# A hybrid attention and recurrence block: the attention output's norm as a step of its own

## The chip, the cores and the metric

The kernel runs on one core of one Trainium2 chip. The metric is the device time of one execution in microseconds (us); less is better. Five engines work side by side on a core, each through its own queue of instructions, in order: TensorE (PE in the profile; the loads of its stationary operand are listed as PEld), VectorE (DVE), ScalarE (ACT), GpSimd (POOL) and SyncE (SP), which here only issues transfers. They wait for each other through semaphores.

## The reference, cut to what matters

One decoder layer for 512 tokens of width 2048, in float32. The input is normalised and projected once; the columns of the projection go to two head groups, eight heads of dilated attention and eight heads of a gated linear recurrence, and the two outputs are concatenated and projected back.

```python
attn = dilated_attention(aq, ak, av).reshape(B, S, ATTN_WIDTH)   # 512 x 1024
attn = rms_norm(attn, attn_out_norm_w)                           # over all 1024 columns of a token

ho = hgrn2(gq, gf, gi, lb)
hg = rms_norm(ho, hg_norm_w) * silu(gg)                          # per head of 128 columns
mix = concatenate([attn, hg], axis=-1) @ w_out                   # 512 x 2048 times 2048 x 2048
x = x + gate1 * mix
# then a second norm and a squared-ReLU MLP of width 8192, gated and added
```

The change concerns the second line, and when it is done beside the lines under it. What is computed stays the same.

## The kernel before

Tokens stand in four tiles of 128 (`NT`), channels in blocks of 128. Float32 products are made as three matmuls of split operands: each weight block is loaded as `wraw`, rounded by ACT into `whi` (L39), and DVE forms the remainder `wlo` (L40); activations are split into `hi` and `lo` in the same way (`split_to`, L239 and L240). Weight tiles are in rings of four buffers: one load brings the rows of two k steps, and a cast can start as soon as PE has finished with the buffer four k steps back.

A projection (`project`) runs 16 k steps. One k step is twelve matmuls of 128x512 (L198 to L200, four token tiles by three products); here it is called a group. After each group `tick()` advances a list of generators, `tasks`, by one `yield`; the head of the list runs until it ends, then the next begins. So the order of PE's instructions is that of the code, and `tasks` is how the work of the heads is dealt out between the groups. PE's queue is recorded as written (`manual_schedule`); the order on ACT, DVE, POOL and SP is set by a planner that goes by its own costs. A second list, `bgw`, runs the adaLN matrix-vector products in the background: transfers `araw` (L123) and DVE instructions L127 and L129.

Near the place of the change the projections are, in order: the gate of the first recurrent half (`hg_gate(0)`), the gate of the second (`hg_gate(1)`), then the output projection in four quarters (`project_out(q)`). While `hg_gate(1)` runs, the list holds the rest of the second attention half, then `hg_out(0)`, then `attention_out`; `hg_out(1)` is appended behind them.

- `hg_out(half)` lets three ticks pass, multiplies the four heads by the gate on DVE (L718, one instruction for each head and token tile) and hands each head to `to_mix`.
- `attention_out` squares and sums the eight tiles `aq` on ACT (L530), adds the partial sums (L531) and makes the reciprocal root on DVE and POOL (L211, L212), multiplies the eight tiles on DVE (L535), then hands eight heads to `to_mix`, one for each tick.
- `to_mix` transposes a head's four blocks on PE into one bank of PSUM (L545, tile `ptm`, a ring of four banks) and writes it to SBUF as a `mix` block on ACT (L547). `mix` blocks are split in the order 8 to 11 (first recurrent half), 0 to 7 (attention), 12 to 15 (second recurrent half) and are consumed in that order by the 16 groups of `project_out(0)`, which asks for two ticks for each of its first ten groups.

The output tiles of the squares (`jk`, L529) are in the same ring of two buffers, tag `ev`, as the tiles `sg` in which `hg_gate` makes its sigmoids (L706 to L709). At the end of `hg_gate(1)` ACT copies the four banks to `gg` (L703), then makes the sigmoids (L707), and DVE finishes them (L708, L709).

Of the kernel before, what the change touches and what calls it, by code (L numbers as in the profile page):

```python
# [44 lines left out]
def hybrid_block(ctx, tc, x, c, positions, norm1_w, w_ada, b_ada, w_in, q_norm_w, k_norm_w,  # L45
# [164 lines left out]
    def rstd_of(dst, ss, n, inv_n):  # L210
        dve.tensor_scalar(dst, ss, inv_n, EPS, op0=ALU.mult, op1=ALU.add)  # L211
        pool.tensor_tensor(dst, dst, mhalf[:, 0:n], op=ALU.pow)  # L212
# [15 lines left out]
    def slot(name, dt=F32):  # L228
        return io.tile([P, 512], dt, name=name, tag="io")
# [124 lines left out]
    tasks = []  # L354
# [13 lines left out]
    def project(c0, mm, rate=1.85, after=None):  # L368

        banks = [bank("prj", tag="mm") for _ in range(4)]  # L370
        for k0 in range(0, NK, 2):
            for j, (whi, wlo) in enumerate(load_w(win_v, k0, c0, 512, None)):
                k = k0 + j
                mm(banks, hhi[k], hlo[k], whi, wlo, k == 0, k == NK - 1)
                tick()
                owed[0] += rate
                while owed[0] >= 1.0:
                    bg_step()
                    owed[0] -= 1.0
                if after:  # L380
                    after(k)
        return banks
# [55 lines left out]
    def qk(c0, name, i):  # L438
        ts = evac(project(c0, tok_mm), name)
        rs = sm.tile([P, NT, 4], F32, name=f"rs{i}", bufs=2)  # L440
        bgw.insert(0, qk_norm(ts, i, rs))
        return ts if i else (ts, rs)
# [78 lines left out]
        values(3, p_sb, lsum)  # L521
        yield

    def attention_out(aos):
        ssa = sm.tile([P, NT, 2], F32, name="ssa", bufs=1)
        ra = sm.tile([P, NT], F32, name="ra", bufs=1)
        for ti in range(NT):
            for u in range(2):
                jk = wk.tile([P, 512], F32, name="jk", tag="ev", bufs=2)  # L529
                act.activation(jk, aos[u][ti], AF.Square, accum_out=ssa[:, ti, u:u + 1])  # L530
        dve.tensor_reduce(ra, ssa, axis=AX.X, op=ALU.add)  # L531
        rstd_of(ra, ra, NT, 1.0 / 1024)
        for u in range(2):
            for ti in range(NT):
                dve.tensor_scalar(aos[u][ti], aos[u][ti], ra[:, ti:ti + 1], None, op0=ALU.mult)  # L535
        yield
        for u in range(2):
            for h in range(4):
                to_mix(u * 4 + h, aos[u], slice(h * DH, (h + 1) * DH), aoc[:, u * 4 + h:u * 4 + h + 1])
                yield  # L540

    def to_mix(k, src, hs, wcol):
        pt = bank("ptm")
        for ti in range(NT):
            pe.transpose(pt[:, ti * P:(ti + 1) * P], src[ti][:, hs], ident)  # L545
        mix[k] = slot("mix")
        act.activation(mix[k], pt, AF.Identity, scale=wcol)  # L547
# [149 lines left out]
    def hg_gate(ht):  # L697
        gb = project(6144 + ht * 512, tok_mm, after=split_early if ht else None)
        gs = []
        for ti in range(NT):  # L700
            g = slot("gg")
            with tc.high_priority():
                act.copy(g, gb[ti])  # L703
            gs.append(g)
        for g in gs:
            sg = wk.tile([P, 512], F32, name="sg", tag="ev", bufs=2)  # L706
            act.activation(sg, g, AF.Tanh, scale=0.5)  # L707
            dve.tensor_scalar(sg, sg, 0.5, 0.5, op0=ALU.mult, op1=ALU.add)  # L708
            dve.tensor_tensor(g, g, sg, op=ALU.mult)  # L709
        return gs  # L710

    def hg_out(ht, gs, os_, rs):
        for _ in range(3):
            yield
        for h in range(4):
            hs = slice(h * DH, (h + 1) * DH)
            for ti in range(NT):
                dve.scalar_tensor_tensor(gs[ti][:, hs], os_[h][:, ti * P:(ti + 1) * P], rs[:, h, ti:ti + 1],  # L718
                                         gs[ti][:, hs], op0=ALU.mult, op1=ALU.mult)
            yield  # L720
            to_mix(8 + ht * 4 + h, gs, hs, hgc)
# [118 lines left out]
    q0 = qk(0, "aq", 0)  # L840
# [6 lines left out]
    q1 = qk(512, "aq", 0)  # L847
    k1 = qk(1024 + 512, "ak", 1)
    v1 = evac(project(2048 + 512, tok_mm), "av")
    tasks.append(attention(q1, k1, v1))  # L850
    gs = hg_gate(0)
    tasks.append(hg_out(0, gs, f0, hrs[0]))
    tasks.append(attention_out((q0[0], q1[0])))
    gs = hg_gate(1)
    tasks.append(hg_out(1, gs, f1, hrs[1]))
# [547 lines left out]
def _program(arrays):  # L1403
    import concourse.bacc as bacc
    nc = bacc.Bacc("TRN2", target_bir_lowering=False, num_devices=1)
    args = [nc.dram_tensor(n, a.shape, mybir.dt.from_np(a.dtype), kind="ExternalInput").ap()
            for n, a in arrays.items()]
    args.append(nc.dram_tensor("out_0_dram", _OUTS[0][0], F32, kind="ExternalOutput").ap())
    with tile.TileContext(nc, schedule_with_timeline_sim=True) as tc:
        hybrid_block(tc, *args)  # L1410
    return nc
# [10 lines left out]
```

## Time and profile before

| what | before |
|---|---|
| time, median of 3 runs | 2303.53 us (2301.55 to 2304.42) |
| the profiled execution's own time | 2298.58 us |
| its span, first to last instruction | 2296.8 us |
| mean granted TensorE clock | 0.993 |
| PE busy | 2227.1 us (97%) |
| DVE busy | 1810.4 us (79%) |
| ACT busy | 1098.4 us (48%) |
| POOL busy | 444.6 us (19%) |

The span is the time between the core's first and last instruction; 1.8 us of the execution's time lie around it. A page shows each engine's busy time, the span in 40 slices with the clock that PE was granted, the transfer queues, and the chain of work that ended last. The answers of the trace that are used below are: stretches of time with the busy time of each engine in them; instructions in order of time, each with its start, its duration and, in square brackets, how long its engine had stood idle before it and what ended that; and the median time of transfers from issue to landing. A line such as L545 is the line of the kernel before; behind the change these lines stand two or three lower.

### The profile page before, as it was taken

To read this page: it belongs to the slowest core of one execution; us is meant where nothing else is said; L and a number is where in the kernel's file an instruction comes from. 1 tells how busy PE (TensorE), PEld (TensorE's weight loads), DVE (VectorE), ACT (ScalarE), POOL (GpSimd) and SP (SyncE) were. 2 spreads that over 40 slices of the span, in tenths; PEclk is the share of its full clock that TensorE was granted. 3 is DMA by queue.
4 is the path that set the end of the run, shared out by engine and by line. 5 is a ranking of instruction groups with operands and counts; after the bars stand their busy time and mean duration, and the time that the engine had idled before them with its cause. 6 is when DMAs were issued, how large, how long until landed. Compare 5 with 4: busy or idle time off the path is not lost.

```text
span 2296.8 us, 33106 instructions
## 1 busy us (share of the span) xinstructions
PE 2227.1 (97%) x11769; PEld 1825.0 (79%) x11769; DVE 1810.4 (79%) x2765; ACT 1098.4 (48%) x1950; POOL 444.6 (19%) x664
## 2 busy tenths in 40 slices
PE   4999999999999979999999999999999999999999
PEld 3787878878778868888887888888888888788887
DVE  6999778678786574678748988988897779967878
ACT  5555434433444453457544656555564333343332
POOL 1000022000220000002232323323333222222221
PEclk9999999999999989999999999999999999999999
DMA  9798455646555256756969799889889987998784
GB/s 327 254 335 316 129 176 166 198 146 219 168 176 157 73 165 198 249 168 214 371 226 383 255 346 351 297 305 384 301 327 388 344 294 261 379 342 293 276 301 165
DMA packets 262583, 598.31 MB, mean 260 GB/s; under 512 B 23221, under 2 KB 43969, under 8 KB 262417
## 3 DMA queue, kind: packets, MB, share of 16 engines
q1 hardware_dynamic: 186800, 332.54, 43.1%
q0 software_dynamic: 70720, 254.21, 30.0%
q10 hardware_dynamic: 4896, 9.44, 1.2%
q8 instruction: 93, 1.52, 0.3%
q14 instruction: 74, 0.60, 0.1%
HBM read 518.49 MB, written 77.61 MB: 260 GB/s over the span
## 4 chain that ended last, share of the span: by engine, by line
PE 63%; issue 15%; DMA 10%; DVE 7%; POOL 2%; ACT 1%; SPq 0%; POOLq 0%; DVEq 0%; ACTq 0%
PE f L1179 8%; PE f L1180 8%; PE f L1178 8%; PE prj L198 8%; PE prj L199 7%; PE prj L200 7%; DMA f_lod<-fs 2%; PE f L208 2%; PE f L207 2%; PE f L206 2%; DVE vlo L1163 2%; DMA araw<-in_w_ada_dram 2%; PE prj L207 2%; PE prj L208 2%; PE prj L206 1%
## 5 line engine op out<-in xcount | busy, mean ns | idle before, releaser
L1162 ACT CAST vhi<-raw 128x1024 fp32r<-128x1024 f32 x392 | 413.5, 1056 | 536.7 <-PE f L1180 415.7
L1163 DVE TENSOR_TENSOR vlo<-raw,vhi 128x1024 fp32r<-128x1024 f32 x392 | 476.9, 1222 | 152.1 <-ACT vhi L1162 151.2
L1179 PE MATMUL f<-vlo,Fh 128*128 128x512 f32 x1376 | 537.5, 391 | 3.4 <-DVE vlo L1163 3.3
L1180 PE MATMUL f<-vhi,Fl 128*128 128x512 f32 x1376 | 535.7, 389 | 0.8 <-DMA Fl<-f_lod 0.8
L1178 PE MATMUL f<-vhi,Fh 128*128 128x512 f32 x1376 | 536.0, 390 | 0.0
L39 ACT CAST whi<-wraw 128x512 fp32r<-128x512 f32 (+1 forms) x368 | 220.2, 601 | 460.3 <-PE prj L200 315.3
L198 PE MATMUL prj<-whi,hi 128*128 128x512 f32 x896 | 366.1, 409 | 3.7 <-ACT gq L562 2.2
L200 PE MATMUL prj<-whi,lo 128*128 128x512 f32 x896 | 352.0, 393 | 0.0
L199 PE MATMUL prj<-wlo,hi 128*128 128x512 f32 x896 | 351.7, 393 | 0.0
L40 DVE TENSOR_TENSOR wlo<-wraw,whi 128x512 fp32r<-128x512 f32 (+1 forms) x368 | 243.5, 666 | 135.0 <-ACT whi L39 132.3
L129 DVE SCALAR_TENSOR_TENSOR acc<-araw,sc,acc 128x512 f32<-128x512 f32 (+1 forms) x392 | 253.6, 675 | 92.9 <-DMA araw<-in_w_ada_dram 91.8
L1179 PEld LDWEIGHTS f<-vlo,Fh 128*128 128x128 f32 x1376 | 258.2, 188 | 63.4 <-DVE vlo L1163 10.4
L1180 PEld LDWEIGHTS f<-vhi,Fl 128*128 128x128 f32 x1376 | 258.3, 188 | 54.4 <-DMA Fl<-f_lod 1.2
L1178 PEld LDWEIGHTS f<-vhi,Fh 128*128 128x128 f32 x1376 | 258.3, 188 | 53.8
L1146 DVE TENSOR_TENSOR raw<-raw,raw 128x1024 f32<-128x1024 f32 x224 | 268.9, 1221 | 3.7 <-DMA raw<-in_w_ff_dram 3.3
L198 PEld LDWEIGHTS prj<-whi,hi 128*128 128x128 f32 x896 | 169.6, 189 | 40.3 <-ACT gq L562 3.8
L200 PEld LDWEIGHTS prj<-whi,lo 128*128 128x128 f32 x896 | 169.4, 189 | 36.9
L199 PEld LDWEIGHTS prj<-wlo,hi 128*128 128x128 f32 x896 | 169.9, 190 | 32.3 <-DVE wlo L40 0.4
L1124 POOL DMA_DIRECT2D Fh<-f_hid x112 | 79.2, 707 | 424.7 <-PE f L1180 408.5
L208 PE MATMUL f<-hi,wlo 128*128 128x512 f32 x256 | 99.9, 390 | 1.6 <-DVE wlo L40 1.6
L206 PE MATMUL f<-hi,whi 128*128 128x512 f32 x256 | 100.3, 392 | 0.0
L207 PE MATMUL f<-lo,whi 128*128 128x512 f32 x256 | 99.6, 389 | 0.0
(311 smaller groups left out, 2917.3 us busy)
## 6 DMA issues: line engine op xcount, KB each, us to landing
raw<-in_w_ff_dram SPq DMA_DIRECT2D x224, 512.0 KB, 9.7
araw<-in_w_ada_dram SPq DMA_DIRECT2D x384, 256.0 KB, 4.2
Fh<-f_hid POOLq DMA_DIRECT2D x112, 512.0 KB, 6.6
Fl<-f_lod POOLq DMA_DIRECT2D x112, 512.0 KB, 7.5
wraw<-in_w_in_dram SPq DMA_DIRECT2D x104, 512.0 KB, 4.2
Fh<-h_hid POOLq DMA_DIRECT2D x60, 512.0 KB, 6.5
Fl<-h_lod POOLq DMA_DIRECT2D x60, 512.0 KB, 7.3
f_hid<-part POOLq DMA_DIRECT2D x48, 512.0 KB, 7.9
```

Of the source, the lines that this page charges most:

```text
L39: nc.scalar.copy(hi, src)
L40: (eng or nc.vector).tensor_tensor(lo, src, hi.bitcast(F32), op=ALU.subtract)
L129: dve.scalar_tensor_tensor(acc, raw[:, k - k0], vec[:, k:k + 1], acc, op0=ALU.mult, op1=ALU.add)
L198: pe.matmul(banks[ti], lhsT=hi[:, ts], rhs=whi, start=first, stop=False)
L199: pe.matmul(banks[ti], lhsT=hi[:, ts], rhs=wlo, start=False, stop=False)
L200: pe.matmul(banks[ti], lhsT=lo[:, ts], rhs=whi, start=False, stop=last)
L1146: dve.tensor_tensor(dst, a, b, op=ALU.subtract)
L1162: act.copy(hi, src)
L1163: split_done.append(dve.tensor_tensor(lo, src, hi.bitcast(F32), op=ALU.subtract))
L1178: pe.matmul(banks[t], lhsT=fh[u][a][:, ts], rhs=whi[:, a], start=first, stop=False)
L1179: pe.matmul(banks[t], lhsT=fh[u][a][:, ts], rhs=wlo[:, a], start=False, stop=False)
L1180: pe.matmul(banks[t], lhsT=fl[u][a][:, ts], rhs=whi[:, a], start=False, stop=end)
```

## The change

The first part of `attention_out`, squares to products, becomes a generator `attention_norm` with one `yield`, queued ahead of `hg_out(0)`. `attention_out` keeps the eight transposes and stays behind `hg_out(0)`.

```diff
-    def attention_out(aos):
+    def attention_norm(aos):
         ssa = sm.tile([P, NT, 2], F32, name="ssa", bufs=1)
         ra = sm.tile([P, NT], F32, name="ra", bufs=1)
         for ti in range(NT):
             for u in range(2):
                 jk = wk.tile([P, 512], F32, name="jk", tag="ev", bufs=2)
                 act.activation(jk, aos[u][ti], AF.Square, accum_out=ssa[:, ti, u:u + 1])
         dve.tensor_reduce(ra, ssa, axis=AX.X, op=ALU.add)
         rstd_of(ra, ra, NT, 1.0 / 1024)
         for u in range(2):
             for ti in range(NT):
                 dve.tensor_scalar(aos[u][ti], aos[u][ti], ra[:, ti:ti + 1], None, op0=ALU.mult)
         yield
+
+    def attention_out(aos):
         for u in range(2):
             for h in range(4):
                 to_mix(u * 4 + h, aos[u], slice(h * DH, (h + 1) * DH), aoc[:, u * 4 + h:u * 4 + h + 1])
                 yield
...
     tasks.append(attention(q1, k1, v1))
     gs = hg_gate(0)
+    tasks.append(attention_norm((q0[0], q1[0])))
     tasks.append(hg_out(0, gs, f0, hrs[0]))
     tasks.append(attention_out((q0[0], q1[0])))
     gs = hg_gate(1)
```

What this does to the queues shows at three places.

The first is DVE's queue around the norm. Before, the norm (`ra`, `aq`) stands behind the whole gate of the second recurrent half (`sg`, `gg`):

```order
L708 TENSOR_SCALAR sg<-sg 128x512 x2
L709 TENSOR_TENSOR gg<-gg,sg 128x512 x2
L40 TENSOR_TENSOR wlo<-wraw,whi 128x512
L718 SCALAR_TENSOR_TENSOR gg<-f,hrs_2102,gg 128x128 x6
...
L718 SCALAR_TENSOR_TENSOR gg<-f,hrs_2102,gg 128x128 x8
L531 TENSOR_REDUCE ra<-ssa 128x4
L211 TENSOR_SCALAR ra<-ra 128x4
L535 TENSOR_SCALAR aq<-aq,ra 128x512 x8
L127 TENSOR_SCALAR acc<-araw,sc 128x512 x2
```

Now, with the same names:

```order
L505 TENSOR_SCALAR aq<-po,lsum 128x128 x4
L40 TENSOR_TENSOR wlo<-wraw,whi 128x512
L531 TENSOR_REDUCE ra<-ssa 128x4
L211 TENSOR_SCALAR ra<-ra 128x4
L40 TENSOR_TENSOR wlo<-wraw,whi 128x512
L535 TENSOR_SCALAR aq<-aq,ra 128x512 x8
L40 TENSOR_TENSOR wlo<-wraw,whi 128x512 x4
L240 TENSOR_TENSOR lo_8702<-mix,hi_8701 128x512
L40 TENSOR_TENSOR wlo<-wraw,whi 128x512
L240 TENSOR_TENSOR lo_8729<-mix,hi_8728 128x512
L710 TENSOR_SCALAR sg<-sg 128x512 x2
L711 TENSOR_TENSOR gg<-gg,sg 128x512 x2
```

The norm follows the last attention head's output (L505) with two weight splits between; the second half's gate begins behind it. The eight squares on ACT move with it, from behind the sigmoids to behind that head.

The second is PE's queue at the end of `hg_gate(1)` and in the first groups of `project_out(0)`. `gg` are the transposes of the first recurrent half, `aq` those of attention. Before:

```order
L545 MATMUL ptm<-ident,gg 128x128 x4
L198 MATMUL prj<-whi,hi_8650 128x512
...
L200 MATMUL prj<-whi,lo_8651 128x512
L545 MATMUL ptm<-ident,gg 128x128 x4
L545 MATMUL ptm<-ident,aq 128x128 x4
L198 MATMUL prj<-whi,hi_8687 128x512
...
L200 MATMUL prj<-whi,lo_8688 128x512
L545 MATMUL ptm<-ident,aq 128x128 x8
```

Now:

```order
L547 MATMUL ptm<-ident,gg 128x128 x4
L198 MATMUL prj<-whi,hi_8701 128x512
...
L200 MATMUL prj<-whi,lo_8702 128x512
L547 MATMUL ptm<-ident,gg 128x128 x8
L547 MATMUL ptm<-ident,aq 128x128 x4
L198 MATMUL prj<-whi,hi_8728 128x512
...
L200 MATMUL prj<-whi,lo_8729 128x512
L547 MATMUL ptm<-ident,aq 128x128 x8
```

The norm's own tick pushes each of the first three heads of `hg_out(0)` back by one group; the fourth head and all of attention's transposes stay where they were. No matmul is added or taken away.

The third is SP's queue of transfers: weights `wraw` of `project_out`, and `araw`, the background product of the second residual gate. Before:

```order
L189 DMA wraw<-in_w_out_dram 128x2x512 x6
L123 DMA araw<-in_w_ada_dram 128x512 x10
L189 DMA wraw<-in_w_out_dram 128x2x512
L123 DMA araw<-in_w_ada_dram 128x512 x7
L189 DMA wraw<-in_w_out_dram 128x2x512
L123 DMA araw<-in_w_ada_dram 128x512 x3
```

Now:

```order
L189 DMA wraw<-in_w_out_dram 128x2x512 x7
L123 DMA araw<-in_w_ada_dram 128x512 x5
L189 DMA wraw<-in_w_out_dram 128x2x512
L123 DMA araw<-in_w_ada_dram 128x512 x5
L189 DMA wraw<-in_w_out_dram 128x2x512
L123 DMA araw<-in_w_ada_dram 128x512 x4
L189 DMA wraw<-in_w_out_dram 128x2x512
L123 DMA araw<-in_w_ada_dram 128x512 x5
```

One more weight load stands ahead of the background transfers, and the two kinds alternate more finely. The first `araw` uses memory of tiles that the stage before gave up: before, it waits among others for the last square (L530) and for the last `gg` of L709; now for the last `gg` alone.

## The prediction

> **What bounds the kernel now.** I read the page first: engine shares and the granted clock.
>
> ```profile
> span 2296.8 us, 33106 instructions
> PE 2227.1 (97%) x11769; PEld 1825.0 (79%) x11769; DVE 1810.4 (79%) x2765; ACT 1098.4 (48%) x1950; POOL 444.6 (19%) x664
> PEclk9999999999999989999999999999999999999999
> ```
>
> PE is busy 97% of the span, so time is won where PE stands still or runs slowly, and nowhere else. One slice after the start has a lower clock, the 15th, about 804 to 861 us: the end of `hg_gate(1)` and the start of `project_out(0)`, where the change works. Next, three stretches around it (length, then busy time and count of PE, PEld, DVE, ACT, POOL, then clock, DMA share, GB/s), and PE in order of time:
>
> ```profile
> 813.00:826.00 13.00, 0.04 (x1) 0.07 (x1) 9.47 (x28) 7.37 (x21) 1.01 (x1) 0.58 0.07 23
> 826.00:856.00 30.00, 30.00 (x141) 24.47 (x142) 25.29 (x44) 16.85 (x29) 0.00 (x0) 0.90 0.73 235
> ```
>
> ```profile
> 807.61 0.60 PE L545 MATMUL ptm<-ident,gg 128*128 128x128 f32 x4
> 809.54 0.50 PE L198 MATMUL prj<-whi,hi 128*128 128x512 f32 x1 [1.33 <-ACT gg L703]
> 812.40 0.60 PE L545 MATMUL ptm<-ident,gg 128*128 128x128 f32 x4
> 825.96 1.57 PE L545 MATMUL ptm<-ident,aq 128*128 128x128 f32 x4 [12.96 <-DVE aq L535]
> 827.19 0.77 PE L198 MATMUL prj<-whi,hi 128*128 128x512 f32 x1
> 832.37 1.04 PE L545 MATMUL ptm<-ident,aq 128*128 128x128 f32 x8
> 849.18 0.60 PE L545 MATMUL ptm<-ident,gg 128*128 128x128 f32 x4
> 849.54 0.48 PE L198 MATMUL prj<-whi,hi 128*128 128x512 f32 x1
> 852.38 1.03 PE L545 MATMUL ptm<-ident,gg 128*128 128x128 f32 x8
> 853.17 0.48 PE L198 MATMUL prj<-whi,hi 128*128 128x512 f32 x1
> ```
>
> PE stands for 12.96 us before the first attention transpose, for the normalised `aq`, and then works from 825.96 to 832.37 at a lower rate. Why `aq` is late stands in DVE's, ACT's and POOL's order of time:
>
> ```profile
> 812.12 0.87 DVE L708 TENSOR_SCALAR sg<-sg 128x512 f32<-128x512 f32 x2
> 812.90 1.29 DVE L709 TENSOR_TENSOR gg<-gg,sg 128x512 f32<-128x512 f32 x2
> 819.28 2.18 DVE L718 SCALAR_TENSOR_TENSOR gg<-f,hrs,gg 128x128 f32<-128x128 f32 x8
> 823.84 0.16 DVE L531 TENSOR_REDUCE ra<-ssa 128x4 f32<-128x8 f32 x1 [2.37 <-ACT jk L530]
> 825.33 3.26 DVE L535 TENSOR_SCALAR aq<-aq,ra 128x512 f32<-128x512 f32 x8 [1.12 <-POOL ra L212]
> 824.28 1.01 POOL L212 TENSOR_TENSOR ra<-ra,mhalf 128x4 f32<-128x4 f32 x1 [123.67 <-DVE ra L211]
> 818.80 0.63 ACT L530 ACTIVATE jk<-aq 128x512 f32<-128x512 f32 x1 [3.44 <-DVE gg L709]
> 823.62 0.19 ACT L530 ACTIVATION_READ_ACCUMULATOR jk<-aq 128x1 f32 x1
> ```
>
> ACT's squares wait for the last L709, a user of the ring `ev`: the norm hangs behind the second half's gate, with which it has no data in common. Then come eight squares (818.80 to 823.81), the reduction, POOL's root, the products. That chain ends the wait.
>
> **The change, part by part.** The sum is made against the profiled execution's 2298.58 us; the median shown, 2303.53, is 4.95 above it. I take the saving off both and forecast a median.
>
> *The wait.* The norm now follows L505 of the last attention head. Here are that place, and the two rhythms there:
>
> ```profile
> 787.77 1.13 DVE L505 TENSOR_SCALAR aq<-po,lsum 128x128 f32<-128x128 f32 x4 [0.89 <-PE po L501]
> 796.60 0.69 DVE L40 TENSOR_TENSOR wlo<-wraw,whi 128x512 fp32r<-128x512 f32 x1 [2.03 <-ACT whi L39]
> 793.22 0.62 ACT L39 CAST whi<-wraw 128x512 fp32r<-128x512 f32 x1 [2.10 <-PE prj L200]
> 795.94 0.62 ACT L39 CAST whi<-wraw 128x512 fp32r<-128x512 f32 x1 [2.10 <-PE prj L200]
> ```
>
> L505 ends at 788.90. Of the squares one can go earlier and seven behind L505: at (823.81 - 818.80) / 8 = 0.63 us each that is 4.4, with two casts of 0.62 between 5.6, so 794.5. The reduction to the end of POOL's root took 825.29 - 823.84 = 1.45, with one weight split 0.69: 796.7. Products 3.26: `aq` is ready at about 800. Its first transposes stand behind group 0 of `project_out(0)`, not before 812. The wait goes whole, with 12 us to spare: **12.96 us**.
>
> *The slow clock behind it.* The four transposes at 825.96 took 1.23 us to the next row, those at 849.18 took 0.36; the group from 827.19 to 832.37 took 5.18, that from 849.54 to 852.38 took 2.84. Loss: 0.87 + 2.34 = **3.21 us**. It goes with the wait, since the 1.33 us wait at 809.54 is not followed by slow rows (from there to 812.40 a group takes 2.86). [...]
>
> *The work put into `hg_gate(1)`.* ACT gets 5.0 us and DVE 0.16 + 0.17 + 3.26 = 3.6. Cover: a weight cast starts when PE frees its buffer (the releaser PE L200 in both L39 rows) and is needed four groups later by the ring of four, less the group in which it is made: three groups of 2.72 us (795.94 - 793.22) = 8.2. DVE stands 2.03 in every 2.72 us. So `whi` comes at most 5.0 late and `wlo` 3.6 later still if the two add in full, 8.6 against 8.2. But two casts stand between the squares, and DVE's idle time absorbs the rest. Nothing; without the cover, at most 0.4. The next weight load, released by `wlo`, is late by as much, with the same lead in hand.
>
> *The three moved heads of `hg_out(0)`.* Twelve transposes go one group later; PE's work is the same. Head 2's `mix` now comes behind group 0 and is wanted by group 2. Rows for the queues in front of it:
>
> ```profile
> 808.91 2.04 ACT L703 COPY gg<-prj 128x512 f32<-128x512 f32 x4
> 810.81 0.66 ACT L239 CAST hi<-mix 128x512 fp32r<-128x512 f32 x1
> 836.72 1.26 ACT L547 ACTIVATE mix<-ptm,cols 128x512 f32<-128x512 f32 x2
> L707 ACT ACTIVATE sg<-gg 128x512 f32<-128x512 f32 x4 | 2.4, 642 | 0.0
> L240 DVE TENSOR_TENSOR lo<-mix,hi 128x512 fp32r<-128x512 f32 x15 | 10.3, 686 | 2.9 <-ACT hi L239 2.9
> ```
>
> (The last two are the groups of 805 to 860 us: busy us, mean ns.) With four transposes fewer ahead of it, 849.54 - 849.18 = 0.36 us, all shifts to 0.36 earlier: group 0 runs from 809.18 to 812.04, eight `gg` and four `aq` transposes (0.79 by 853.17 - 852.38, and 0.36) to 813.19, group 1 (2.84) to 816.03, eight transposes to 816.82. Group 2 wants the split remainder of head 2 in its third matmul, about 817.4. DVE: the split of head 1 ends at 811.84 (ACT's cast ends 811.11, plus 0.69); then two L708 (0.87), two L709 (1.29), a weight split (0.69), eight L718 (2.18), one L708 (0.42) and head 2's split (0.69), less some 0.08 overlap at each of six joins: 811.84 + 6.14 - 0.5 = 817.5. ACT is earlier: cast for a weight at 812.24, two L547, one L707, the cast of head 2 at about 815.2. A new wait of 0.1; bounds 0 (DVE a little ahead) and 2.84 (one whole group late). Taken **0.5 us**, near the worked value.
>
> *Behind it.* The second half's gate (L708, L709, L718) now runs under PE's groups instead of in the wait, and its transposes are wanted at 849.18 - 15.7 = 833.5. Behind 817.5 DVE has six splits (0.69), one L708, two L709 and eight L718 to the last of that gate, 8.0 less the overlaps: about 825. What is late next is the background product. Its transfers in 820 to 862 us with their landing time, the end of its first block on DVE, and the copies that follow project_out(0):
>
> ```profile
> 823.88 9.74 SPq L123 DMA_DIRECT2D araw<-in_w_ada_dram  x10
> araw<-in_w_ada_dram SPq DMA_DIRECT2D x24, 256.0 KB, 3.4
> 848.27 0.69 DVE L143 TENSOR_TENSOR acc<-acc 128x512 f32<-128x512 f32 x1
> 873.67 2.63 ACT L927 COPY x<-prj 128x512 f32<-128x512 f32 x4
> ```
>
> Half-way through those 8.0, at about 821, the last L709 ends, so `araw` starts only 3 us earlier than before, while PE is 16 earlier. First block 848.27 - 823.88 = 24.4 us: it ends at 845.5. Before the weight split for group 14 stand L143 (0.69), one L127, one L129 and at worst a landing: at most 4.5 later, 850. PE wants it two groups of 2.72 before the end of project_out(0), which falls near 873.6 - 15.7 = 857.9: at 852.4. **0 us**, slack 2.4.
>
> Sum: 12.96 + 3.21 - 0.5 = **15.7 us**. Profiled execution 2298.58 - 15.7 = 2282.9; median 2303.53 - 15.7 = **2288** rounded.
>
> **Rivals.**
>
> *DVE becomes the bound.* From 813 to 856 DVE was busy 9.47 + 25.29 = 34.8 us; less the norm's 3.6 it has 31.2 to do, and PE's work there, 43 - 12.96 - 3.21, is 26.8. For: DVE's queue is in order, and late splits stop PE. Against: eleven of those us are L129, which nothing on PE wants, and splits are 8.2 ahead. If the lead does not count, 31.2 - 26.8 = 4.4 us come back: gain 11.3 to 11.8, time 2292.
>
> *The gain is swallowed later.* The MLP moves data at a DMA share near 0.9; were its transfers the bound, an earlier start would wait for them.
>
> ```profile
> 1200.00:1400.00 200.00, 197.86 (x898) 162.52 (x898) 182.40 (x184) 109.03 (x124) 62.88 (x92) 1.00 0.87 319
> 1600.00:2000.00 400.00, 398.50 (x1776) 328.65 (x1775) 338.79 (x343) 179.04 (x191) 112.72 (x160) 1.00 0.89 329
> raw<-in_w_ff_dram SPq DMA_DIRECT2D x224, 512.0 KB, 9.7
> ```
>
> PE is idle there 2.1 us in 200 and 1.5 in 400, so they are not. If it held, the change would do nothing for the time: 2303.5.
>
> *Slower: the background product stops PE.* In DVE's queue L129 waits for `araw` ahead of weight splits, and SP's new order puts weight loads between. Five rounds of the ring of four `araw` fall before group 14. Each us above the 3.4 us landing costs 5, from a slack of 2.4: loss from 3.9 us on, the whole gain gone from 3.4 + (2.4 + 15.7) / 5 = 7.0. At the 9.7 us of the MLP's loads: 5 x 6.3 - 2.4 - 15.7 = 13.4 slower, 2317. Against: the page's median for all `araw`, the first stages with their fuller queues among them, is 4.2, which costs 5 x 0.8 - 2.4 = 1.6, and DMA's share is 0.73 here.
>
> ```profile
> araw<-in_w_ada_dram SPq DMA_DIRECT2D x384, 256.0 KB, 4.2
> ```
>
> **How the numbers follow.** Forecast 0.62 (14 to 17.5 saved, the upper end with the 1.33 us wait gone too: 2286 to 2289.5); DVE the bound 0.20; swallowed 0.08; slower 0.06; something between or a larger gain 0.04, counted as faster. A measurement can tell some 0.2%, 4.6 us, from no change: faster 0.86, same 0.08, slower 0.06. The range takes the first two cases, with the 1.5 to 2 us by which the three runs differ: 2284 to 2296.
>
> **What would show it.** Right: the squares end and L535 starts before 800; the first `aq` transpose follows the `gg` transposes without a wait, none at half clock; the slices' clock row shows 9 throughout after the start; idle time in front of L545 falls from 13.0 to under 1; `project_out(0)` ends 15 to 16 us earlier and the rest of the span keeps its length. Wrong: waits of L198 to L200 for `lo` or `wlo` of several us between 813 and 860, a second dip of the clock, L129 waiting for `araw` in front of a late L40, or a longer MLP.

## The result, and the profile after

The changed kernel takes **2284.45 us** (median of six runs, 2282.08 to 2286.92), the kernel before 2301.16 us in six runs on the same chip: a ratio of 0.9929 with a 95% interval of 0.9915 to 0.9944, 16.7 us faster. The forecast was 2288 in a range of 2284 to 2296, so the median lies just inside the lower end. The profiled execution of the changed kernel took 2285.62 us, against 2298.58 before.

Its page, engine shares and granted clock:

```profile
span 2283.5 us, 33098 instructions
PE 2225.3 (97%) x11769; PEld 1825.0 (80%) x11769; DVE 1809.0 (79%) x2765; ACT 1098.0 (48%) x1950; POOL 443.2 (19%) x664
PEclk9999999999999999999999999999999999999999
```

The busy times are those of before within 2 us; what is gone is mostly standing time. The dip in the 15th slice of the clock is gone too. The two stretches that were 0.04 of 13 us and 30.00 at clock 0.90 before, in the same columns (length, busy time and count of PE, PEld, DVE, ACT, POOL, clock, DMA share, GB/s):

```profile
813.00:826.00 13.00, 13.00 (x74) 10.85 (x73) 13.00 (x32) 11.93 (x23) 0.00 (x0) 1.00 0.30 100
826.00:856.00 30.00, 30.00 (x144) 24.91 (x143) 23.52 (x38) 12.99 (x22) 0.00 (x0) 1.00 0.85 288
```

PE now works through both at full clock, and DVE is busy without a gap in the first: the second half's gate runs under PE's groups there. PE in order of time at the place of the old wait, and the one weight load that waits:

```profile
809.50 0.50 PE L198 MATMUL prj<-whi,hi 128*128 128x512 f32 x1 [1.33 <-ACT gg L705]
...
812.37 1.03 PE L547 MATMUL ptm<-ident,gg 128*128 128x128 f32 x8
813.25 0.60 PE L547 MATMUL ptm<-ident,aq 128*128 128x128 f32 x4
...
817.84 0.19 PEld L200 LDWEIGHTS prj<-whi,lo 128*128 128x128 f32 x1 [0.33 <-DVE lo L240]
```

The first `aq` transposes at 813.25 follow the `gg` transposes without a wait. The bracket on L198 was there before, and the 0.33 us for `lo` is new. The norm itself, on ACT and DVE:

```profile
788.60 0.63 ACT L530 ACTIVATE jk<-aq 128x512 f32<-128x512 f32 x1 [2.00 <-DVE aq L505]
...
793.56 0.16 DVE L531 TENSOR_REDUCE ra<-ssa 128x4 f32<-128x8 f32 x1 [0.54 <-ACT jk L530]
...
795.04 3.26 DVE L535 TENSOR_SCALAR aq<-aq,ra 128x512 f32<-128x512 f32 x8
```

The squares now wait for L505, on which they depend, instead of for a gate's product, and `aq` is ready at 798.3, 15 us ahead of 813.25.

Single executions differ by a few us before and behind the place of the change. The comparison below therefore uses one measure from the traces, the **stretch** from the first product of the last attention head (L505) to the start of the copies of `project_out(0)`'s result (L927, now L930). Its two ends in the changed kernel:

```profile
788.22 1.13 DVE L505 TENSOR_SCALAR aq<-po,lsum 128x128 f32<-128x128 f32 x4 [0.89 <-PE po L501]
...
857.95 2.63 ACT L930 COPY x<-prj 128x512 f32<-128x512 f32 x4
```

Before it was 873.67 - 787.77 = 85.90 us, now 857.95 - 788.22 = 69.73: **16.17 us** shorter. All kernels of this study follow, with the rest of the span from the start of those copies on, and the time as a ratio to runs of the kernel before on the same chip (the medians come from several chips). `ring` has only the squares' output in another ring; `heads` is the change without the moved heads, `moved` the moved heads alone; the three `fill` kernels give PE idle work in the wait; `norm2` and `norm3` do the norm twice and three times; `dve_load` adds work on DVE; `bg_banks` and `ring_banks` start `project_out(0)` in other banks.

| kernel | stretch, us | gain in it | rest of the span | median, us | ratio (95%) |
|---|---|---|---|---|---|
| before | 85.90 | | 1423.1 | 2301.16 | |
| the change | 69.73 | 16.17 | 1425.6 | 2284.45 | 0.9929 (0.9915 to 0.9944) |
| ring | 69.57 | 16.33 | 1424.2 | 2285.10 | 0.9937 (0.9925 to 0.9950) |
| heads | 69.51 | 16.39 | 1425.9 | 2284.89 | 0.9933 (0.9920 to 0.9945) |
| moved | 83.40 | 2.50 | 1428.1 | 2297.45 | 0.9991 (0.9982 to 1.0000) |
| fill | 83.54 | 2.36 | 1424.2 | 2298.64 | 0.9991 (0.9982 to 1.0000) |
| norm2 | 69.70 | 16.20 | 1424.7 | 2284.71 | 0.9937 (0.9923 to 0.9950) |
| norm3 | 74.16 | 11.74 | 1430.0 | 2292.11 | 0.9969 (0.9958 to 0.9979) |
| dve_load | 69.95 | 15.95 | 1427.5 | 2284.70 | 0.9935 (0.9920 to 0.9950) |
| bg_banks | 70.01 | 15.89 | 1425.7 | 2286.44 | 0.9943 (0.9931 to 0.9956) |
| fill21 | 85.87 | 0.03 | 1426.0 | 2302.39 (one run) | |
| fill14 | 85.83 | 0.07 | 1425.8 | 2300.24 (one run) | |
| ring_banks | 68.21 | 17.69 | 1425.7 | 2281.90 | 0.9915 (0.9901 to 0.9929) |

The rest of the span goes from 1423.1 to 1430.0 in single executions, so differences of a us or two there say nothing about an edit. The stretch repeats well where nothing should change in its length: 85.90, 85.87 and 85.83 in three kernels, 69.73 and 69.70 in two.

### The profile page after: what moved, and what is told of

Its sections match the earlier page's. It is cut to its first block, busy times and chain, and to the rows that moved or that the text cites. A ratio compares the mean times of both kernels' runs of the same rounds, so it can differ in the third digit from the quotient of the medians.

```text
span 2283.5 us, 33098 instructions
## 1 busy us (share of the span) xinstructions
PE 2225.3 (97%) x11769; PEld 1825.0 (80%) x11769; DVE 1809.0 (79%) x2765; ACT 1098.0 (48%) x1950; POOL 443.2 (19%) x664
## 4 chain that ended last, share of the span: by engine, by line
PE 67%; issue 12%; DMA 11%; DVE 7%; POOL 3%; ACT 1%; SPq 0%; POOLq 0%; DVEq 0%; ACTq 0%
PE prj L198 9%; PE prj L200 9%; PE prj L199 8%; PE f L1183 8%; PE f L1182 8%; PE f L1181 8%; DMA f_lod<-fs 3%; PE f L208 2%; PE f L206 2%; PE f L207 2%; DMA f_hid<-part 2%; PE prj L207 2%; DVE vlo L1166 2%; PE prj L208 2%; DMA araw<-in_w_ada_dram 1%
## 5 line engine op out<-in xcount | busy, mean ns | idle before, releaser
L198 PE MATMUL prj<-whi,hi 128*128 128x512 f32 x896 | 365.1, 408 | 3.8 <-ACT gq L564 2.4
L200 PE MATMUL prj<-whi,lo 128*128 128x512 f32 x896 | 351.3, 392 | 0.0
L198 PEld LDWEIGHTS prj<-whi,hi 128*128 128x128 f32 x896 | 169.0, 189 | 40.0 <-ACT gq L564 3.8
L200 PEld LDWEIGHTS prj<-whi,lo 128*128 128x128 f32 x896 | 169.0, 189 | 37.0 <-DVE lo L240 0.3
```

Source lines behind the costliest of these rows:

```text
L198: pe.matmul(banks[ti], lhsT=hi[:, ts], rhs=whi, start=first, stop=False)
L200: pe.matmul(banks[ti], lhsT=lo[:, ts], rhs=whi, start=False, stop=last)
```

## The experiments

### What held the norm: the ring alone

Theory: the squares waited for a buffer of the gate's ring, and the order that the planner made from that put the norm behind the gate. The edit gives the squares' output another ring and touches nothing else; no step and no head is moved.

```diff
-                jk = wk.tile([P, 512], F32, name="jk", tag="ev", bufs=2)
+                jk = work("jk")
                 act.activation(jk, aos[u][ti], AF.Square, accum_out=ssa[:, ti, u:u + 1])
```

> The kernel before with one edit: the eight squares of attention's norm write their (unused) output tile into the ring `wk` instead of the ring `ev`, which the sigmoids of the gate use. The source order, PE's order and the places of all heads are those of before; on DVE the norm now stands behind L505 as in the changed kernel. Theory (the norm hung on the shared ring and on what the planner made of it, and its early place is the whole gain): no wait of PE for `aq`, clock full, 16 us gone at that place, time as the changed kernel or up to 0.5 us better, since no head is moved: about 2284. Rival 1 (the moved heads or the new order of transfers bring part of the gain): slower than the changed kernel by that part, 2287 or more. Rival 2 (the ring is only one of several things that hold the norm): still near 2301.

The norm's products on DVE, and PE behind the first group of `project_out(0)`, in this kernel:

```profile
796.22 3.25 DVE L535 TENSOR_SCALAR aq<-aq,ra 128x512 f32<-128x512 f32 x8
...
811.28 0.50 PE L198 MATMUL prj<-whi,hi 128*128 128x512 f32 x1 [1.33 <-ACT gg L703]
...
814.57 0.60 PE L545 MATMUL ptm<-ident,aq 128*128 128x128 f32 x4
```

PE's order is that of before, and the wait for `aq` is gone all the same. Stretch 69.57 us, gain 16.33; time 2285.1, as the changed kernel within the intervals. The ring was what held the norm: one tag gives the whole gain, and neither the step of its own nor the moved heads are needed for it. Rival 2 falls, and of rival 1 the moved heads. The order of SP's transfers came out new here too (five `araw` ahead of the next weight load instead of ten), so this run does not separate it; but the wait and the slow rows, 12.96 + 3.21 = 16.17 us, leave it next to nothing of the 16.33.

### The moved heads: taken out, and alone

In the first kernel the heads of `hg_out(0)` go back to their old groups:

```diff
     def hg_out(ht, gs, os_, rs):
-        for _ in range(3):
+        for _ in range(3 if ht else 2):
             yield
```

> The changed kernel, but hg_out(0) waits two steps instead of three, so that the heads of the first recurrent half stand in the same groups as before the change. It takes the moved heads out of the change. Theory: they cost what PE waits in group 2 of project_out(0), 0.1 to 0.5 us in the prediction and 0.33 us in the trace of the changed kernel, so 2284.1 against 2284.45, not to be told apart by the time, and the 0.33 us wait of L200's weights for `lo` is gone in the trace. Rival (moving the heads is what lets the gate's work run under PE): the time goes up by 2 us or more, to 2287 or above.

Stretch 69.51 us, time 2284.89. The wait of L200's weights for `lo` is gone. Against this and the ring, the changed kernel's 69.73 is 0.16 to 0.22 longer: that is the price of the moved heads, too small for the times to show.

The second kernel moves the heads and leaves the norm where it was (before, with `range(3 if ht else 4)` at the same place):

> The kernel before, with hg_out(0) waiting four steps instead of three and the norm left in attention_out: the moved heads alone. Attention's first transposes come one group later as well, so PE has one group of 2.84 us more ahead of the same wait. Theory: the norm still hangs behind the second half's gate and is ready at the same time, about 826; the wait shrinks to about 10.1 us, the slow rows stay: 2301.2 - 2.8 = 2298.4. Rival (the moved heads are the gain): 2290 or less. Rival (the heads that come later hold the groups behind them): no change or slower, 2301 or more.

PE's first `aq` transposes and the next ones behind a group:

```profile
827.65 2.43 PE L545 MATMUL ptm<-ident,aq 128*128 128x128 f32 x8 [10.95 <-DVE aq L535]
829.73 0.78 PE L198 MATMUL prj<-whi,hi 128*128 128x512 f32 x1
...
834.08 1.03 PE L545 MATMUL ptm<-ident,aq 128*128 128x128 f32 x8
```

The wait is 10.95 us where 10.1 was expected, the stretch 2.50 shorter where 2.8 was, the time 2297.45 (ratio 0.9991). PE does one more group ahead of the same wait and then stands. The moved heads bring no more than that.

### The slow rows behind the wait: 3.21 us, but of two kinds

The prediction put 3.21 us down to the clock: 0.87 at the four transposes and 2.34 in the group behind them. Here PE gets idle work through the wait:

```diff
         pt = bank("ptm")
+        for _ in range(31 if k == 0 else 0):
+            for ti in range(NT):
+                pe.transpose(pt[:, ti * P:(ti + 1) * P], ident, ident)
         for ti in range(NT):
             pe.transpose(pt[:, ti * P:(ti + 1) * P], src[ti][:, hs], ident)
```

> The kernel before, plus 124 transposes of the identity on PE, 31 times four, ahead of attention's first head, into the bank that this head then overwrites. At 0.79 us for eight they last 12.3 us and fill the wait of 12.96 us almost whole, so PE has work through it but gains nothing from it. The prediction's term of 3.21 us (slow clock behind the wait): all of it goes, the four `aq` transposes take 0.36 us and the group behind them 2.84: 2301.2 - 3.2 = 2298. Rival 1: the 0.87 us at the four transposes is the pace of DVE's products, one in 0.41 us, and no matter of the clock; then they still take about 1.2 us and only 2.34 us go: 2298.8. Rival 2 (the low clock comes from something other than the idle spell): rows stay slow, 2301.

PE and its weight loads in this kernel (L548 is the line of the transposes here, L546 the added ones):

```profile
814.28 13.70 PE L546 MATMUL ptm<-ident 128*128 128x128 f32 x124
827.81 1.02 PE L548 MATMUL ptm<-ident,aq 128*128 128x128 f32 x4
828.11 0.14 PEld L548 LDWEIGHTS ptm<-ident,aq 128*128 128x128 f32 x1 [0.15 <-DVE aq L535]
828.50 0.14 PEld L548 LDWEIGHTS ptm<-ident,aq 128*128 128x128 f32 x1 [0.26 <-DVE aq L535]
828.59 0.48 PE L198 MATMUL prj<-whi,hi 128*128 128x512 f32 x1
...
831.45 0.82 PE L548 MATMUL ptm<-ident,aq 128*128 128x128 f32 x6
```

The group behind the transposes takes 831.45 - 828.59 = 2.86 us, the full rate (2.86 from 809.54 and 2.84 from 849.54 before), and the granted clock from 813.5 to 850 us is 1.00 where it was 0.51 from 826 to 832.4 us before: here the low clock does come from the idle spell. The time is 2298.64 us, ratio 0.9991 (0.9982 to 1.0000), too near to before to tell 2.3 from 3.2 us; the stretch tells them apart. It is 2.36 us shorter, not 3.21, and two of the four transposes still wait, at full clock, for a product. They take 0.78 us and not 1.23 only because the added work ends after the first product is ready; counted from L505 the row behind them starts at 828.59 - 789.21 = 39.38 us here and at 827.19 - 787.77 = 39.42 before. The same brackets stand in the trace of before, PE's weight loads behind the 12.96 us:

```profile
826.66 0.18 PEld L545 LDWEIGHTS ptm<-ident,aq 128*128 128x128 f32 x1 [0.21 <-DVE aq L535]
827.06 0.18 PEld L545 LDWEIGHTS ptm<-ident,aq 128*128 128x128 f32 x1 [0.21 <-DVE aq L535]
```

The loads come 0.40 us apart, the pace of the eight products in 3.26 us. So 0.87 of the 3.21 us is no clock at all: it is the tail of the wait, four transposes that follow DVE's products one by one. Rival 1 of this run holds, and the clock's part is 2.34 us.

Two more kernels, with 21 and 14 rounds of the same transposes instead of 31, leave PE standing for part of the wait.

> As the run with 124 transposes of the identity ahead of attention's first head, but 84 of them: at the 13.70 us that 124 took they last 9.3 us, so PE stands about 3.8 us before `aq` comes. It asks only what an idle spell of this length does to the rows behind it. Theory of the prediction (the low clock comes from the idle spell): slow rows if 3.8 us are enough; the group behind the four `aq` transposes takes 2.84 us if not and up to 5.18 if so. 1.33, 2.33 and 2.63 us were not enough in other runs, 10.95 and 12.96 were. Time between 2298 and 2301.

> The same with 56 transposes, 6.2 us, so PE stands about 6.9 us before `aq` comes. Slow rows expected: a group of 4 to 5.2 us behind the four `aq` transposes; if it takes 2.84, the spell must be longer than 6.9 us. Time between 2298 and 2301.

PE with 21 rounds:

```profile
826.85 1.66 PE L548 MATMUL ptm<-ident,aq 128*128 128x128 f32 x4 [3.70 <-DVE aq L535]
828.16 0.78 PE L198 MATMUL prj<-whi,hi 128*128 128x512 f32 x1
...
833.31 1.04 PE L548 MATMUL ptm<-ident,aq 128*128 128x128 f32 x8
```

PE with 14 rounds:

```profile
824.96 1.66 PE L548 MATMUL ptm<-ident,aq 128*128 128x128 f32 x4 [6.75 <-DVE aq L535]
826.28 0.78 PE L198 MATMUL prj<-whi,hi 128*128 128x512 f32 x1
...
831.37 1.04 PE L548 MATMUL ptm<-ident,aq 128*128 128x128 f32 x8
```

The group behind takes 5.15 us after a spell of 3.70, 5.09 after 6.75 and 5.18 after 12.96. The price is nearly the same in these three, 2.31, 2.25 and 2.34 us above 2.84: it does not grow with the spell. The single time with 21 rounds, 2302.39, lies above the expected 2301, but the kernel before took 2302.32 on that chip. Both kernels have the stretch of before (85.87 and 85.83), since PE only did something useless in a wait whose end is set by DVE.

### How much room the norm has

The changed kernel with all of the norm between the two tiles' allocation and the `yield` in a loop, twice, and three times:

```diff
     def attention_norm(aos):
...
+        for _ in range(2):
             for ti in range(NT):
...
         yield
```

> The changed kernel with the whole norm done twice in its step, squares, reduction, root and products (the second pass finds rows of mean square 1 and changes them by rounding alone). Added: 5.0 us on ACT, 3.6 on DVE, one root on POOL, and a chain of some 9 to 10.7 us, so `aq` is ready at 807.5 to 809 instead of 798.3 and is wanted at 813.25. Theory (12 us to spare, and weight splits covered by their lead): no wait of PE, the time stays within 0.5 us of 2284.45. Rival (the work put into hg_gate(1) is only just hidden): the second pass costs from 3.6 (DVE's share) to 8.6 us, 2288 to 2293, with waits of PE for `wlo` between 790 and 812.

DVE's second products and PE's first `aq` transposes in the kernel with two norms:

```profile
804.08 3.26 DVE L536 TENSOR_SCALAR aq<-aq,ra 128x512 f32<-128x512 f32 x8 [0.28 <-POOL ra L212]
...
813.65 0.60 PE L548 MATMUL ptm<-ident,aq 128*128 128x128 f32 x4
```

`aq` is ready at 807.3, PE wants it at 813.65, and the stretch is 69.70 us against 69.73. A whole second norm, which put the products back by 8.6 us (804.08 against 795.47 for the first pass), costs nothing: the room holds that much, and the cover of the weight splits stands.

> The changed kernel with the norm done three times. `aq` is ready at 817 to 820, its first four columns' tiles some 1.6 us earlier, and it is wanted at 813.25. Theory: PE waits 4 to 6.5 us, then 0.87 us at the pace of the products; whether slow rows follow an idle spell of that length (2.34 us behind 12.96, none behind 1.33) is open: 5 to 9.7 us more, 2289.5 to 2294. Rival 1 (the slack is larger than worked out): 2285. Rival 2 (DVE's gate work, pushed behind the third pass, becomes the bound): further waits of PE for `lo` or `wlo` of several us, 2295 or more.

PE in order of time in the kernel with three:

```profile
813.09 0.50 PE L198 MATMUL prj<-whi,hi 128*128 128x512 f32 x1 [2.33 <-ACT gg L706]
...
819.61 1.43 PE L548 MATMUL ptm<-ident,aq 128*128 128x128 f32 x4 [2.63 <-DVE aq L536]
820.80 0.48 PE L198 MATMUL prj<-whi,hi 128*128 128x512 f32 x1
...
823.63 1.03 PE L548 MATMUL ptm<-ident,aq 128*128 128x128 f32 x8
...
876.74 0.50 PE L199 MATMUL prj<-wlo,hi 128*128 128x512 f32 x1 [1.33 <-DVE wlo L40]
```

The third pass no longer fits. The wait for `aq` was expected at 4 to 6.5 us and is 2.63: PE goes on at 819.61, 0.63 us after the first of the eight products begins (818.98) and 2.63 before the last one ends (822.24), and it comes 1.0 us later itself, because ACT's squares now stand ahead of the gate's copies (2.33 us instead of 1.33). The four transposes follow the products (1.19 us; three of the four weight loads wait for one, 0.7 us together). The group behind takes 823.63 - 820.80 = 2.83: neither 2.33 nor 2.63 us of standing brought slow rows. The stretch is 4.43 us longer. The time is 7.7 us longer (7.4 against two norms on the same chip), inside the expected 5 to 9.7, though the wait was outside its range. Behind the stretch the profiled execution has three waits for `wlo` between 876 and 960 us, 1.9 us together, that the changed kernel does not have (the longest is the last row); the cause of the rest is open.

### Whether DVE is the bound

Eight more products in the second half's gate, whose results nobody reads:

```diff
             dve.tensor_tensor(g, g, sg, op=ALU.mult)
+            for _ in range(2 if ht else 0):
+                dve.tensor_tensor(sg, g, sg, op=ALU.mult)
         return gs
```

> The changed kernel with eight more products of 0.65 us on DVE in the second half's gate, two for each tile, into the sigmoid's tile, which nobody reads afterwards: 5.2 us of DVE work more in the stretch in which DVE was busy 13.00 of 13 us (813 to 826) and 23.52 of 30 (826 to 856). The planner puts six of them around heads' splits and moves the gate's last products (L720) back. Theory (DVE has idle time left behind 826, splits lead by several us, the gate's products are wanted only at 833.5): at most 1 us, 2284.5 to 2285.5. Rival (DVE is the bound of project_out(0) now): the 5.2 us come out in full, 2289.7.

The same two stretches of time in this kernel, and PE's only new wait:

```profile
813.00:826.00 13.00, 13.00 (x78) 11.17 (x77) 12.98 (x28) 12.09 (x23) 0.00 (x0) 1.00 0.13 41
826.00:856.00 30.00, 29.79 (x142) 24.50 (x141) 23.74 (x44) 13.45 (x23) 0.00 (x0) 1.00 0.67 228
...
834.70 0.33 PE L547 MATMUL ptm<-ident,gg 128*128 128x128 f32 x1 [0.21 <-DVE gg L722]
```

The stretch is 0.22 us longer, the time 2284.7: DVE is not the bound. But the reason given was not the one. DVE's busy time from 813 to 856 is 36.72 us, with 5.2 us added, against 36.52. The time comes from the background product, which slides back: DVE's work on `araw` in 826 to 856 falls from 12.35 us (18 instructions) to 8.05 (12), and DMA's share from 0.85 to 0.67. The gate's products, wanted at 833.5, are now just late, by 0.21 us. The slack is work that can be put off, not idle time.

### The wait that is left

Of the waits in the stretch 1.33 us remain, at the start of `project_out(0)`, for ACT's copy of a bank that `hg_gate(1)` holds. In the changed kernel the first two banks are taken from the other ring:

```diff
-        banks = [bank("prj", tag="bg" if q % 2 and i < 2 else "mm") for i in range(4)]
+        banks = [bank("prj", tag="bg" if q % 2 == 0 and i < 2 else "mm") for i in range(4)]
```

> The changed kernel with one edit in project_out: the first two banks of its accumulators come from the other ring of banks in the even column blocks instead of the odd ones, so project_out(0) begins in two banks that hg_gate(1) does not hold. Theory: its first matmul no longer waits 1.33 us for ACT's copy of the gate's first bank; nothing else moves: 2283.1 against 2284.45. Rival (two of the four banks in which the transposes of the heads are made are then held through project_out(0), and the transposes wait for ACT's `mix`): waits of PE in front of ptm of 0.5 us or more a group, slower than the changed kernel.

PE's transposes behind the first group of `project_out(0)` in this kernel:

```profile
811.80 1.03 PE L547 MATMUL ptm<-ident,gg 128*128 128x128 f32 x8
814.44 0.66 PE L547 MATMUL ptm<-ident,aq 128*128 128x128 f32 x4 [1.60 <-ACT mix L549]
```

The rival came true at one place. The 1.33 us are gone, but three heads stand behind group 0 here, two of `gg` and one of `aq`, and only two banks are left for them: the third waits 1.60 us for ACT to empty one. Stretch 70.01, 0.28 longer. Of the three heads one is there because the change moved it. So the same edit was put on the kernel with the other ring, in which no head is moved:

> The kernel before with two edits: the squares' output tile in the ring `wk`, and the first two banks of project_out's even column blocks from the other ring of banks. No head is moved, so behind group 0 stand one head of the recurrent half and one of attention, two banks, and no third one that would have to wait for ACT's `mix`. Theory: both waits go, 1.33 us at the start of project_out(0) and 12.96 for `aq`; from the first L505 of the last attention head to the copies behind project_out(0) 69.57 - 1.33 = 68.2 us, time about 2283. Rival (with two of four banks held, the transposes wait for ACT here as well): 69.8 us or more, 2285.

The two ends of the stretch in that kernel, and PE's first `aq` transposes between:

```profile
788.18 1.13 DVE L505 TENSOR_SCALAR aq<-po,lsum 128x128 f32<-128x128 f32 x4 [0.89 <-PE po L501]
...
811.89 0.60 PE L545 MATMUL ptm<-ident,aq 128*128 128x128 f32 x4
...
856.39 2.63 ACT L927 COPY x<-prj 128x512 f32<-128x512 f32 x4
```

Stretch 856.39 - 788.18 = 68.21 us, as expected, and no wait of a PE matmul is left in it. With 2281.9 us, ratio 0.9915 (0.9901 to 0.9929), it is the fastest kernel here: 17.69 us gained in the stretch with two edited lines of the kernel before. Its interval overlaps with that of the change (0.9915 to 0.9944), and each was timed against other runs of the kernel before, so the times alone do not settle its lead of 2.6 us; the 1.5 us by which its stretch is shorter stand in the trace.

## Why the prediction was right

**The wait, 12.96 us.** Right, place and size. `aq` was ready at 798.3 where about 800 was worked out, and PE wanted it at 813.25, so the room was 15 us where 12 had been worked out. The runs with two and three norms agree but only bracket it: one more norm, 8.6 us, fits, two do not.

**The slow clock, 3.21 us.** The sum was right and its name half wrong. 2.34 us were the clock (2.36 with PE kept busy); the 0.87 at the four transposes were DVE's pace of products (with three norms, where the group behind shows no slow row at 2.83 us, the same four take 1.19 us, against 1.23 before). Both go when the norm is early, so the total did not suffer. The mistake came from reading matmul rows alone; PE's weight loads carried the brackets that tell the two apart.

**The work put into `hg_gate(1)`, nothing.** Right: even twice the work costs nothing there.

**The moved heads, 0.5 us.** Right in kind, too dear: the wait for head 2's `lo` is 0.33 us at a weight load and 0.16 to 0.22 in the stretch; 0.1 had been worked out. The transposes of the second half, expected at 833.5, begin at 833.47.

**Behind it, 0 us.** No wait came, as forecast, but the slack was worked out from a wrong place. The page's view of transfers in 820 to 862 us, DVE at the end of the first block and the split for group 14, and the first matmul of that group that uses it:

```profile
araw<-in_w_ada_dram SPq DMA_DIRECT2D x23, 256.0 KB, 4.3
...
847.00 0.69 DVE L143 TENSOR_TENSOR acc<-acc 128x512 f32<-128x512 f32 x1
...
848.91 0.69 DVE L40 TENSOR_TENSOR wlo<-wraw,whi 128x512 fp32r<-128x512 f32 x1
...
854.58 0.39 PE L199 MATMUL prj<-wlo,hi 128*128 128x512 f32 x1
```

`araw` landed in 4.3 us instead of 3.4, and the block ended at 847.7, 2.2 later than forecast. Between the block and the end of the split lay 1.9 us, where at most 4.5 had been allowed, so the split was done at 849.6, near the 850 worked out: two errors that cancelled. The need at 852.4 was misplaced. The prediction took the first copy (L927) for the end of `project_out(0)`, but the copies start 0.9 us into its last group, as soon as the first bank is done (857.95, the group from 857.07). PE wanted the split at 854.6, and the slack was 5.0 us, not 2.4. Nor did the slower rival's rate hold: 0.9 us of landing should have made the block 4.5 us longer, and it took 26.5 us instead of 24.4.

**The sum.** 15.7 forecast; 16.17 in the stretch, 16.7 between the medians; the stretch gained 0.5 more than forecast, mostly because the moved heads cost 0.16 to 0.22 and not 0.5. 2.4 of the 3.4 us by which 2287.8 was too high come from the median of three runs before (2303.53) against six (2301.16).

**The rivals.** DVE as the bound: refuted by eight more products. Swallowed later: no. The rest of the span varies by up to 7 us from one execution to another and does not grow as the stretch shrinks. In the changed kernel's profiled execution it is 2.4 us longer than in that of before, partly through one slow spell shown below; so these two lie only 12.96 us apart (by chance the size of the wait), the medians 16.7. The slower case did not come.

What the prediction did not see is how little of the change was needed. It named the shared ring as what the squares waited for, and never asked whether a different ring would do alone.

## To carry to other kernels

When an operation stands behind work with which it shares no data, look for a shared buffer first: here two buffers of scratch output, never read, held a norm back and cost 16 us, and another tag was worth as much as the new order. After a wait, read the weight loads with the matmuls before you call slow rows a clock: if they wait for single results, as two of four did here for 0.21 us each, they are the wait's tail. Before you free a bank or a slot for one wait, count who uses the ring it comes from in the next few us; the same line lost 0.28 us on one order and gained 1.36 on the other.

## What the runs showed of the hardware

The price of a spell of standing did not grow with its length here. Behind 1.33, 2.33 and 2.63 us no row was slow (the next group took 2.86, 2.86 and 2.83 us); behind 3.70, 6.75 and 12.96 the next group took 5.1 to 5.2 us instead of 2.84. Behind the 10.95 us of the kernel with the moved heads alone it took only 4.35 (834.08 - 829.73): eight transposes stood in front of it instead of four, and the slow rows ended within it. From the first work to the last slow row it lasted 6.4 us (before), 6.5 (21 rounds), 6.2 (14 rounds) and 5.5 (moved heads), so the loss also hung on what work fell into that time. And length alone does not decide whether it comes. In the changed kernel's profiled execution, in the MLP, slow rows followed two short waits in a row:

```profile
1964.07 0.50 PE L1181 MATMUL f<-vhi,Fh 128*128 128x512 f32 x1 [0.93 <-ACT vhi L1165]
...
1965.33 0.50 PE L1182 MATMUL f<-vlo,Fh 128*128 128x512 f32 x1 [0.76 <-DVE vlo L1166]
...
1965.94 0.63 PE L1181 MATMUL f<-vhi,Fh 128*128 128x512 f32 x1
...
1968.93 0.53 PE L1182 MATMUL f<-vlo,Fh 128*128 128x512 f32 x1
1969.30 0.40 PE L1183 MATMUL f<-vhi,Fl 128*128 128x512 f32 x1
```

PE did one matmul in 2.2 us there, and then seven steps of 0.43 us where 0.23 is usual, up to 4.0 us after the second wait; the granted clock from 1966 to 1970 was 0.60. Why these 2.2 us were followed by slow rows and the 2.63 us with three norms were not, no run here shows.
